# Attention keys, queries and weights turned by VectorE through DRAM instead of by TensorE

## The chip, the cores and the metric

The program runs on one core of a Trainium2 chip. The metric is the device time of one execution in microseconds, the median of three runs. One profiled execution of the kernel before gives the trace. The engines are TensorE (PE in the profile, with its weight loads as PEld), VectorE (DVE), ScalarE (ACT), GpSimd (POOL) and SyncE (SP). DMAs are issued from the queues of SP and ACT here.

## The reference

A context of 256 tokens and 256 latent tokens, width 2048, float32, two layers. What the change touches is the attention of the first layer, and the adaptive sums of both:

```python
def adaln(cond, w, b):
    m = jax.nn.silu(cond) @ w + b            # w is 2048 x 6144: one vector times a matrix
    return jnp.split(m, 3, axis=-1)
...
q = rms_norm(heads(cols(p, COL_Q, NA_WIDTH, 0), NA_HEADS, NA_HEAD_DIM), q_norm_g)   # 16 heads of 128
k = rms_norm(heads(cols(p, COL_K, NA_WIDTH, 0), NA_HEADS, NA_HEAD_DIM), k_norm_g)
...
s_lat = jnp.einsum('bqhd,bkhd->bhqk', qr, kb).astype(jnp.float32) * scale + bias.astype(jnp.float32)
s_ctx = jnp.einsum('bqhd,bkhd->bhqk', qr, k_ctx).astype(jnp.float32) * scale
pr = jax.nn.softmax(jnp.concatenate([s_lat, s_ctx], axis=-1), axis=-1).astype(v.dtype)
return (jnp.einsum('bhqk,bkhd->bqhd', pr[..., :kh * GRID_W], vb)
        + jnp.einsum('bhqk,bkhd->bqhd', pr[..., kh * GRID_W:], v_ctx))
...
ya = ya * jax.nn.silu(cols(p, COL_GATE_A, NA_WIDTH, 0))
```

Beside it the first layer has a state-space part (SSD) with a group norm; both go through one output projection, the second layer is a gated short convolution, and each layer ends with `x + gate * y`.

## The kernel before, in words

Nearly all of the work is projections. A float32 weight block of 128 x 1024 is loaded into one of five `raw` buffers by a DMA on the SP queue (`issue`), ScalarE casts it to a rounded high part `wH` (`split`, L423), VectorE subtracts to get the low part `wL` (`low_part`, L430), and TensorE multiplies high by high, high by low and low by high. There are three `wH`/`wL` pairs, so the split runs at most three blocks ahead of TensorE. `give_raw` hands a `raw` buffer back when its block is split, and the next load goes out.

The attention runs beside the projections in four groups `a` of four heads. `kq_gen` normalizes keys (4 tiles of 128 tokens x 4 heads of 128) and queries (2 tiles), and turns each 128 x 128 piece on TensorE (`turn`, L202: a matmul against the identity into a PSUM bank), from where ScalarE copies it to `KT` or VectorE, times `gqk`, to `QT`. `head_gen` makes scores with the splits `kH`, `kL`, `qH`, `qL`, adds the bias and takes the maximum in `top`, takes the exponential on ScalarE, scales by the sum in `scale_`, turns the weights of each 128 queries on TensorE in `trans` (4 pieces), splits them into `PH`, `PL`, and multiplies by the values. `put_mix` writes the head's output to DRAM (`mixd`), and `mix_gen` reads pairs of outputs back and splits them for the output projection.

`gemv_gen` forms the adaptive vectors: 16 blocks of 512 columns, each summed in `acc` by VectorE from 8 loads of `ada_w` (two operations of 128 x 512 each, L820), then summed over partitions by TensorE and written to `mrow`. These loads use the same SP queue and the same `raw` buffers as the weights. `res_gen` forms `x + gate * y` after the output projection, and `turn_gen` turns the result on TensorE.

The second layer already turns two tensors through DRAM: a tile is written with its 32 x 32 blocks reordered (`mixed`, `plain`), `fetch` reads it back in four DMAs on the ACT queue (L212) so that each block lands on its partitions, and `blocks` turns every 32 x 32 block on VectorE (L217). These are the tiles `Du` and `Dg` from the DRAM tensor `trd`.

The order of all instructions is fixed when the program is built. Tasks are generators in three lists (`urgent`, `side`, `back`); each yields a wait, `W_(engine, tiles, banks)`, and `pump` runs a task on when `may` says that by the planner's clock (`Plan`) its inputs are ready. `Plan.add` gives every instruction a start and an end by a table of costs; `when` waits for a condition, `("grow", t, h)` and `("cap", t, h)` take and return temporary buffers. "AQ" stands for a DMA on the ACT queue. The planner's clock only sets the order: on the chip each engine runs its own list in order and waits on semaphores. A DMA's issue waits too, in its queue.

Of the kernel before, what the change touches and what calls it, by code (L numbers as in the profile page):

```python
# [8 lines left out]
F32 = mybir.dt.float32  # L9
# [28 lines left out]
class Plan:  # L38
# [59 lines left out]
    def add(self, b):  # L98
# [8 lines left out]
        for k in ko:  # L107
            s = max(s, 0.0 if e == "PE" else self.w[k] + 60, self.r[k] + 60)
        if op == "DMACopy":
# [20 lines left out]
        for k in ko:  # L130
            self.w[k] = done
            self.last[k[0]] = max(self.last[k[0]], done)
# [9 lines left out]
def kernel(ctx: ExitStack, tc, x, cx, ada_w, ada_b, w_in, w_out, sc_in, sc_out, rpb, small, const,  # L142
# [120 lines left out]
    def may(task, hor, isurg):  # L263
# [48 lines left out]
    def force(ok, qs=(urgent, side)):  # L312

        pump()
        while not ok():
            best = None
            for q in qs:
                for task in list(q):
# [10 lines left out]
                    else:  # L329
                        if len(free_b) < nb:  # L330
                            continue
                        when_ = max(plan.t["ACT" if eng == "AQ" else eng], plan.ready(f))
# [472 lines left out]
    def gemv_gen():  # L805
        for n in range(16):
            lay = 0 if n < 4 else 1
            c0 = 4096 + n * 512 if n < 4 else (n - 4) * 512
            yield W_("DVE", nb=0)
            E(V.memset(acc, 0.0))  # L810
            E(DMA.dma_start(acc[:1, :], ada_b[lay:lay + 1, c0:c0 + 512]))
            for k in range(8):
                yield when(lambda: not (("gem", n, k) not in RAW))
                yield W_("DVE", RAW["gem", n, k][1], acc)
                raw, v = RAW.pop(("gem", n, k))
                ngem[0] -= 1
                for j in range(2):
                    if j:
                        yield W_("DVE", acc)
                    E(V.scalar_tensor_tensor(out=acc, in0=v[:, j], scalar=csil[:, 2 * k + j:2 * k + j + 1], in1=acc,  # L820
# [8 lines left out]
            E(V.tensor_copy(rowb, ps[:, :128]))  # L829
# [15 lines left out]
    rowb = mrb = st([128, 128], "rowb")  # L845

# [88 lines left out]

    def put_mix(i, o):
        yield W_("AQ", o)
# [7 lines left out]
    attn = [0]  # L945

    def kq_gen(key, a, ps, nt, stat, dst, banked):
# [10 lines left out]
        kns = {}  # L958

        def norm(t):  # L960
            kn = kns[t] = tmp()
            E(V.tensor_tensor(out=four(kn), in0=ps[t].rearrange("p (h d) -> p h d", h=4),
                              in1=stat[:, 4 * t:4 * t + 4].unsqueeze(2).to_broadcast([128, 4, 128]), op=ALU.mult))
            if banked:
                give(free_b, ps[t])

        for t in range(nt):
            yield W_("DVE", stat)
            norm(t)
        yield when(lambda: not (attn[0] < 8 * (a if key else 0)))  # L970
        for t in range(nt):
            yield W_("PE", kns[t], nb=1)
# [3 lines left out]
            give(free_t, kns[t])  # L976
            yield W_("ACT" if key == "K" else "DVE", pt)
            if key == "K":
                E(S.copy(dst[:, :, t * 128:(t + 1) * 128], four(pt)))
            else:  # L980
                E(V.tensor_scalar(out=dst[:, :, t * 128:(t + 1) * 128], in0=four(pt), scalar1=gqk, scalar2=None, op0=ALU.mult))
            give(free_b, pt)
# [24 lines left out]
    PH, PL = (st([128, 4, 256], f"PT{k}", F32R, name=f"P{'HL'[k]}") for k in range(2))  # L1007
# [4 lines left out]
    def head_gen(a, h):  # L1012
# [21 lines left out]
        def top(qt, ps):  # L1034
# [6 lines left out]
            E(S.activation(sp, sp, AF.Exp, bias=s4[:, 2 + qt:3 + qt], scale=1.0, accum_out=s4[:, 4 + qt:5 + qt]))  # L1041

        def scale_(qt):
            sp = sps[qt]
            E(V.reciprocal(s4[:, 6 + qt:7 + qt], s4[:, 4 + qt:5 + qt]))
            E(V.tensor_scalar(out=sp, in0=sp, scalar1=s4[:, 6 + qt:7 + qt], scalar2=0.5, op0=ALU.mult, op1=ALU.mult))

        def trans(qt):
            pt = bank()
            for kt in range(4):  # L1050
                turn(pt[:, kt * 128:(kt + 1) * 128], sps[qt][:, kt * 128:(kt + 1) * 128])
            give(free_t, sps[qt])
            return pt

        yield when(lambda: ("K", a) in got and ("Q", a) in got and (hd == 0 or ("qk", hd - 1) in got))
        yield ("grow", 2, 0)
        yield W_("ACT", KT[:, h, :], QT[:, h, :])
        E(S.copy(kH, KT[:, h, :]))
        E(S.copy(qH, QT[:, h, :]))
# [869 lines left out]
```

## Time and profile before

| what | value |
|---|---|
| median of three runs | 1801.51 us (1799.98 to 1804.06) |
| the profiled execution | 1802.22 us, its span 1800.3 us |
| busy, of the span | TensorE 98%, VectorE 71%, ScalarE 44%, GpSimd 2% |
| moved from and to HBM | 385.23 MB, mean 214 GB/s |
| granted TensorE clock | 0.998 |

A row of grouped instructions reads: line, engine, operation, output<-inputs, shapes, count | busy us, mean ns of one | idle us of the engine just before them, and what ended it. A row of a timeline reads: start, length, engine, line, operation, output<-input, shape, count, and in brackets the idle time before it with what ended it. A row of a table by stretch reads: stretch, length, then for each engine busy us and count, the granted TensorE clock, the share of time that the 16 DMA engines were busy, GB/s.

### The profile page before, as it was taken

The page shows a single profiled execution, that of the slowest core. Times are in us where ns is not written, and L with a number is a line of the kernel's source. Part 1 is how long each engine was busy: PE and PEld are TensorE (multiplying, and loading weights), DVE is VectorE, ACT ScalarE, POOL GpSimd, SP SyncE. Part 2 cuts the span into 40 slices and gives each one's busy share as a digit, 9 for nine tenths or more (in the row PEclk, how much of TensorE's full clock was granted, in tenths as well). Part 3 has the DMA queues.
Part 4 walks back from the last instruction along what each step waited for, and adds up shares of the span by engine and source line. Part 5 has one row for each costly group of instructions (what it writes and reads, how often), then busy time and mean ns, then how long its engine had stood idle before and what let it go on. Part 6 is the DMA issues. An engine that isn't in the chain of part 4 may idle for free.

```text
span 1800.3 us, 25545 instructions
## 1 busy us (share of the span) xinstructions
PE 1760.2 (98%) x9545; PEld 1469.2 (82%) x9545; DVE 1283.5 (71%) x2049; ACT 785.7 (44%) x1354; POOL 31.1 (2%) x28
## 2 busy tenths in 40 slices
PE   6999999999999999999999999999999999999998
PEld 4677888889888879888878898788877888878887
DVE  5566777878686867685875787787657777767555
ACT  5323544436252455242454343554445444434442
POOL 0000100001000000000001000000000000000000
PEclk9999999999999999999999999999999999999999
DMA  9987654576656556655574566768757888878774
GB/s 347 340 291 254 194 168 126 156 206 194 211 161 190 162 174 204 191 158 167 172 219 120 163 188 194 232 209 295 273 184 232 260 278 268 270 237 265 220 220 167
DMA packets 260220, 385.23 MB, mean 214 GB/s; under 512 B 33424, under 2 KB 113008, under 8 KB 260096
## 3 DMA queue, kind: packets, MB, share of 16 engines
q1 hardware_dynamic: 239792, 366.64, 64.8%
q10 hardware_dynamic: 20304, 16.96, 3.1%
q8 instruction: 75, 1.23, 0.3%
q14 instruction: 49, 0.40, 0.1%
HBM read 372.89 MB, written 11.96 MB: 214 GB/s over the span
## 4 chain that ended last, share of the span: by engine, by line
PE 89%; DMA 4%; DVE 4%; issue 1%; ACT 1%; SPq 0%; POOL 0%; ACTq 0%; POOLq 0%; DVEq 0%
PE bank L198 86%; PE bank L202 3%; DMA raw<-in_ada_w 2%; DVE wL L430 2%; DMA tmp<-dram_csr 1%; DVE acc L820 0%; DMA raw<-in_w_in 0%; DMA Dg<-dram_trd 0%; ACT wH L423 0%; DMA tmp<-in_x 0%; DMA xs<-in_x 0%; DVE hL L769 0%; DVE tmp L1398 0%; DVE tmp L1217 0%; DMA Du<-dram_trd 0%
## 5 line engine op out<-in xcount | busy, mean ns | idle before, releaser
L423 ACT CAST wH<-raw 128x1024 fp32r<-128x1024 f32 (+1 forms) x440 | 459.5, 1045 | 707.4 <-PE bank L198 606.5
L430 DVE TENSOR_TENSOR wL<-raw,wH 128x1024 fp32r<-128x1024 f32 (+1 forms) x440 | 530.5, 1212 | 225.9 <-ACT wH L423 224.1
L198 PE MATMUL bank<-hH,wH 128*128 128x256 f32 (+1 forms) x1040 | 342.7, 330 | 0.9 <-ACT wH L423 0.9
L198 PE MATMUL bank<-hL,wH 128*128 128x256 f32 (+1 forms) x1040 | 336.8, 324 | 0.0
L198 PE MATMUL bank<-hH,wL 128*128 128x256 f32 (+1 forms) x1024 | 331.3, 324 | 1.5 <-DVE wL L430 1.5
L198 PE MATMUL bank<-wH,h 128*128 128x512 f32 x1024 | 318.7, 392 | 2.1 <-DVE h L1662 1.7
L198 PE MATMUL bank<-wH,hH 128*128 128x512 f32 x640 | 257.2, 402 | 4.8 <-ACT hH L763 2.6
L820 DVE SCALAR_TENSOR_TENSOR acc<-raw,csil,acc 128x512 f32<-128x512 f32 x256 | 191.7, 749 | 91.0 <-DMA raw<-in_ada_w 74.0
L198 PE MATMUL bank<-wL,hH 128*128 128x512 f32 x640 | 249.8, 391 | 0.3 <-DVE wL L430 0.3
L198 PE MATMUL bank<-wH,hL 128*128 128x512 f32 x640 | 249.5, 390 | 0.1
L198 PEld LDWEIGHTS bank<-wH,h 128*128 128x128 f32 x1024 | 193.0, 189 | 44.3 <-DVE h L1662 3.0
L198 PEld LDWEIGHTS bank<-hH,wH 128*128 128x128 f32 x1040 | 197.6, 190 | 18.7 <-issue 2.0
L198 PEld LDWEIGHTS bank<-hL,wH 128*128 128x128 f32 x1040 | 197.7, 190 | 15.6
L198 PEld LDWEIGHTS bank<-hH,wL 128*128 128x128 f32 x1024 | 194.5, 190 | 17.8 <-DVE wL L430 2.5
L198 PE MATMUL bank<-wL,h 128*128 128x512 f32 x512 | 200.7, 392 | 5.4 <-DVE wL L430 5.4
L198 PE MATMUL bank<-wH,mix 128*128 128x512 f32 x512 | 162.7, 393 | 0.0
L198 PEld LDWEIGHTS bank<-wH,hH 128*128 128x128 f32 x640 | 120.2, 188 | 35.3 <-issue 6.5
L198 PEld LDWEIGHTS bank<-wH,hL 128*128 128x128 f32 x640 | 120.1, 188 | 25.6 <-DVE hL L769 0.6
L198 PEld LDWEIGHTS bank<-wL,hH 128*128 128x128 f32 x640 | 120.2, 188 | 24.8 <-DVE wL L430 1.1
L198 PEld LDWEIGHTS bank<-wL,h 128*128 128x128 f32 x512 | 96.6, 189 | 27.1 <-DVE wL L430 6.9
L198 PEld LDWEIGHTS bank<-wH,mix 128*128 128x128 f32 x512 | 96.1, 188 | 20.8 <-issue 0.9
L198 PE MATMUL bank<-wL,mix 128*128 128x512 f32 x256 | 99.8, 390 | 0.0
(257 smaller groups left out, 1754.4 us busy)
## 6 DMA issues: line engine op xcount, KB each, us to landing
raw<-in_w_in SPq DMA_DIRECT2D x209, 512.0 KB, 3.8
raw<-in_ada_w SPq DMA_DIRECT2D x163, 512.0 KB, 4.7
raw<-in_sc_in SPq DMA_DIRECT2D x128, 512.0 KB, 4.4
raw<-in_w_out SPq DMA_DIRECT2D x64, 512.0 KB, 4.8
raw<-in_sc_out SPq DMA_DIRECT2D x32, 512.0 KB, 4.6
tmp<-dram_csr SPq DMA_DIRECT2D x32, 256.0 KB, 6.2
PT<-in_ada_w SPq DMA_DIRECT2D x14, 512.0 KB, 8.0
yi<-in_ada_w SPq DMA_DIRECT2D x8, 512.0 KB, 7.4
```

The costliest lines, as they stand in the source:

```text
L198: E(T.matmul(o, l, r, start=start, stop=stop, skip_group_check=True))
L202: E(T.transpose(o, i, ident if k == 128 else ident[:k, :k]))
L423: E(S.copy(H, v))
L430: E(V.tensor_tensor(out=Lo, in0=v, in1=H.bitcast(F32), op=ALU.subtract))
L820: E(V.scalar_tensor_tensor(out=acc, in0=v[:, j], scalar=csil[:, 2 * k + j:2 * k + j + 1], in1=acc, op0=ALU.mult, op1=ALU.add))
```

## The change

Keys, queries and attention weights are no longer turned on TensorE. `kq_gen` writes each normalized tile, blocks reordered, to a new DRAM tensor `kqd`, fetches two tiles at a time into `PT0` and turns the blocks on VectorE straight into `KT` and `QT`. In `head_gen` the exponential is written with its blocks reordered, ScalarE does the scaling by the sum, both tiles go to `ptd` in DRAM and come back in one `fetch` into the same `PT0` (one user at a time, `dfree`), VectorE turns them in place, and `PH`, `PL` are made by one instruction each of 128 x 1024. `gqk` moves into the making of `qH`, `qL`, and the factor 0.5 into the product with the gate. In the group norm the matmul of ones against a scaled identity (`dg`) becomes a `turn` of a broadcast column. `put_mix` keeps an output in SBUF where its place is already free. The adaptive sums start by a product instead of a memset, and the bias `ada_b` is added at the end from `adab`. In the planner a DMA from or to DRAM tensors of the program is put down as 3 us longer, and a wait marked "+" (the adaptive sums, the turns, the splits of `mix_gen`) asks for 1 us more than the plan's ready time. `res_gen` starts only when all heads and groups are done.

```diff
@@ Plan.add
+            if any(a.tensor.name.startswith("dram") for a in ins + outs):
+                done = free = done + 3000
...
@@ may
+        late = eng[-1] == "+"
+        eng = eng.rstrip("+")
...
-        rdy = plan.ready(aps)
+        rdy = plan.ready(aps) + (1000 if late else 0)
...
@@ gemv_gen
-            yield W_("DVE", nb=0)
-            E(V.memset(acc, 0.0))
-            E(DMA.dma_start(acc[:1, :], ada_b[lay:lay + 1, c0:c0 + 512]))
+            yield W_("SP")
+            E(DMA.dma_start(adab[0:128:32, :], ada_b[lay, c0:c0 + 512].rearrange("(g c) -> g c", g=4)))
...
-                yield W_("DVE", RAW["gem", n, k][1], acc)
+                yield W_("DVE+", RAW["gem", n, k][1])
...
+                    if not k + j:
+                        E(V.tensor_scalar(out=acc, in0=v[:, j], scalar1=csil[:, 0:1], scalar2=None, op0=ALU.mult))
+                        continue
...
-            E(V.tensor_copy(rowb, ps[:, :128]))
+            E(V.tensor_tensor(out=rowb, in0=ps[:, :128], in1=adab, op=ALU.add))
...
@@ kq_gen
+            E(V.tensor_tensor(out=mixed(kn), in0=plain(ps[t]),
+                              in1=stat[:, 4 * t:4 * t + 4].unsqueeze(2).unsqueeze(3).to_broadcast([128, 4, 4, 32]), op=ALU.mult))
...
+            yield W_("AQ", kn)
+            E(DMA2.dma_start(src[t * 128:(t + 1) * 128], kn))
...
-            pt = bank()
-            for h in range(4):
-                turn(pt[:, h * 128:(h + 1) * 128], kns[t][:, h * 128:(h + 1) * 128])
...
-                E(S.copy(dst[:, :, t * 128:(t + 1) * 128], four(pt)))
...
-                E(V.tensor_scalar(out=dst[:, :, t * 128:(t + 1) * 128], in0=four(pt), scalar1=gqk, scalar2=None, op0=ALU.mult))
...
+        for t in range(0, nt, 2):
+            yield when(lambda: dfree[0])
+            Dk = d_take(f"kqD_{key}{a}{t}")
+            yield W_("AQ", src[t * 128:(t + 2) * 128])
+            fetch(Dk, src[t * 128:(t + 2) * 128])
+            for k in range(2):
+                yield W_("DVE+", Dk)
+                blocks(dst[:, :, (t + k) * 128:(t + k + 1) * 128], Dk[:, k])
+            dfree[0] = True
...
@@ head_gen
-            E(V.tensor_scalar(out=sp, in0=sp, scalar1=s4[:, 6 + qt:7 + qt], scalar2=0.5, op0=ALU.mult, op1=ALU.mult))
-
-        def trans(qt):
-            pt = bank()
-            for kt in range(4):
-                turn(pt[:, kt * 128:(kt + 1) * 128], sps[qt][:, kt * 128:(kt + 1) * 128])
...
+            E(S.mul(sps[qt], sps[qt], s4[:, 6 + qt:7 + qt]))
+            yield W_("AQ", sps[qt])
+            E(DMA2.dma_start(ptd[hd, qt * 128:(qt + 1) * 128], sps[qt]))
...
+        Dt = d_take(f"D{hd}")
...
+        fetch(Dt, ptd[hd])
+        for qt in range(2):
+            yield W_("DVE+", Dt)
+            turned = Dt[:, qt].rearrange("p (a k j) -> p a k j", a=4, k=4)
+            E(V.transpose(turned, turned))
...
-            mm(po[:, :256], vH[:, ks], PH[:, kt, :], kt == 0, False)
+            mm(po[:, :256], vH[:, ks], PH[:, :, kt, :], kt == 0, False)
...
@@ group_gen
-            mm(Rb[:, t * 128:(t + 1) * 128], ONES, dg[:, t * 128:(t + 1) * 128], t == 0, True)
+            turn(Rb[:, t * 128:(t + 1) * 128], r2[:, t:t + 1].to_broadcast([128, 128]))
```

How the rows move is shown at three places. A row names the line, the operation, output<-inputs with buffer numbers, the shape and how often it stands in succession.

First, TensorE while it projects the gate of head group 2 (`hH`, `hL` are the activations, `wH`, `wL` the weights, `tmp` the normalized keys). Before:

```order
L202 MATMUL bank4_127<-const_153,tmp0_104 128x128 x4
L198 MATMUL bank6_129<-hH10_1128,wH1_137 128x256
L198 MATMUL bank6_129<-hL10_1133,wH1_137 128x256
L198 MATMUL bank6_129<-hH10_1128,wL1_140 128x256
L198 MATMUL bank6_129<-hH10_1128,wH1_137 128x256
L198 MATMUL bank6_129<-hL10_1133,wH1_137 128x256
L198 MATMUL bank6_129<-hH10_1128,wL1_140 128x256
L202 MATMUL bank7_130<-const_153,tmp2_106 128x128 x4
L202 MATMUL bank3_126<-const_153,tmp7_111 128x128 x4
L198 MATMUL bank5_128<-hH11_1135,wH1_137 128x256
L198 MATMUL bank5_128<-hL11_1140,wH1_137 128x256
L198 MATMUL bank5_128<-hH11_1135,wL1_140 128x256
```

The same block of weights after the change:

```order
L200 MATMUL bank5_128<-hH10_1129,wH1_137 128x256
L200 MATMUL bank5_128<-hL10_1134,wH1_137 128x256
L200 MATMUL bank5_128<-hH10_1129,wL1_140 128x256
L200 MATMUL bank5_128<-hH10_1129,wH1_137 128x256
L200 MATMUL bank5_128<-hL10_1134,wH1_137 128x256
L200 MATMUL bank5_128<-hH10_1129,wL1_140 128x256
L200 MATMUL bank6_129<-hH11_1136,wH1_137 128x256
L200 MATMUL bank6_129<-hL11_1141,wH1_137 128x256
L200 MATMUL bank6_129<-hH11_1136,wL1_140 128x256
L200 MATMUL bank6_129<-hH11_1136,wH1_137 128x256
```

The turns are gone and nothing stands in their place; in the whole program TensorE's turns of `tmp` go from 324 to 100.

Second, ScalarE's list at the keys of group 2, where the copies from PSUM to `KT` stood before:

```order
L979 COPY KT_142<-bank3_126 128x4x128
L423 CAST wH0_136<-raw4_135 128x1024
L979 COPY KT_142<-bank4_127 128x4x128
L979 COPY KT_142<-bank7_130 128x4x128
L979 COPY KT_142<-bank3_126 128x4x128
L1058 CAST kH_1687<-KT_142 128x512
L1059 CAST qH_1691<-QT_143 128x256
```

After the change the queue holds four writes to `kqd` and two fetches of four DMAs between the casts of weights:

```order
L996 DMA dram_kqd_1683<-tmp3_107 128x512
L996 DMA dram_kqd_1683<-tmp2_106 128x512
L427 CAST wH1_137<-raw1_132 128x1024
L996 DMA dram_kqd_1683<-tmp6_110 128x512
L427 CAST wH2_138<-raw4_135 128x1024
L427 CAST wH0_136<-raw3_134 128x1024
L996 DMA dram_kqd_1683<-tmp4_108 128x512
L214 DMA kqD_K20_5892<-dram_kqd_1683 32x8x128 x4
L1024 ACTIVATE tmp7_111<-bank6_129 128x512
L1024 ACTIVATE tmp1_105<-bank5_128 128x512
L427 CAST wH1_137<-raw1_132 128x1024
L427 CAST wH2_138<-raw4_135 128x1024
```

VectorE's list for the same fetch after the change:

```order
L434 TENSOR_TENSOR wL0_139<-raw3_134,wH0_136 128x1024
L826 SCALAR_TENSOR_TENSOR acc_219<-raw0_131,csil_160,acc_219 128x512 x2
L1026 SCALAR_TENSOR_TENSOR gt_145<-tmp7_111,bank6_129 128x512
L1026 SCALAR_TENSOR_TENSOR gt_145<-tmp1_105,bank5_128 128x512
L434 TENSOR_TENSOR wL1_140<-raw1_132,wH1_137 128x1024
L835 TENSOR_TENSOR rowb_220<-bank0_123,adab_221 128x128
L219 STREAM_TRANSPOSE KT_142<-kqD_K20_5892 128x4x4x32 x2
L434 TENSOR_TENSOR wL2_141<-raw4_135,wH2_138 128x1024
```

The turn of the fetched tile stands one split behind the block (`wH0`) that ScalarE cast just ahead of the fetch and ahead of the split of `wL2`.

Third, VectorE in the second layer, where the third tile `Du` is turned (at 1595 us in the trace of before). Before:

```order
L810 MEMSET acc_219 128x512
L430 TENSOR_TENSOR wL1_140<-raw1_132,wH1_137 128x1024
L820 SCALAR_TENSOR_TENSOR acc_219<-raw3_134,csil_160,acc_219 128x512 x2
L430 TENSOR_TENSOR wL2_141<-raw2_133,wH2_138 128x1024
L820 SCALAR_TENSOR_TENSOR acc_219<-raw2_133,csil_160,acc_219 128x512 x2
L430 TENSOR_TENSOR wL0_139<-raw4_135,wH0_136 128x1024
L430 TENSOR_TENSOR wL1_140<-raw0_131,wH1_137 128x1024
L430 TENSOR_TENSOR wL2_141<-raw1_132,wH2_138 128x1024
L217 STREAM_TRANSPOSE u_10728<-Du2_12257 128x4x4x32 x2
```

After:

```order
L826 SCALAR_TENSOR_TENSOR acc_219<-raw3_134,csil_160,acc_219 128x512
L434 TENSOR_TENSOR wL2_141<-raw1_132,wH2_138 128x1024
L826 SCALAR_TENSOR_TENSOR acc_219<-raw3_134,csil_160,acc_219 128x512
L434 TENSOR_TENSOR wL0_139<-raw0_131,wH0_136 128x1024
L434 TENSOR_TENSOR wL1_140<-raw4_135,wH1_137 128x1024
L434 TENSOR_TENSOR wL2_141<-raw2_133,wH2_138 128x1024
L826 SCALAR_TENSOR_TENSOR acc_219<-raw3_134,csil_160,acc_219 128x512 x2
L434 TENSOR_TENSOR wL0_139<-raw1_132,wH0_136 128x1024
L434 TENSOR_TENSOR wL1_140<-raw0_131,wH1_137 128x1024
L219 STREAM_TRANSPOSE u_10688<-Du2_12207 128x4x4x32 x2
```

Before, `raw2` is freed by the split of `wL2` and its next load is used by the very next row, so that row has to wait for a whole load. After, three splits stand between the last use of `raw3` and the sum on its next load.

More of the change, by code (lines that the diff above doesn't have):

```diff
@@ L934, with place @@
     mixd = drt([32, 128, 256], "mixd")
-    def put_mix(i, o):
+    mH = [None] * 32
+    def place(i, o):
+        hl = st([128, 2, 256], f"hH{i}" if i < 16 else f"hL{i - 16}", F32R, name=f"mix{i}")
+        E(S.copy(hl[:, 0], o))
+        E(V.tensor_tensor(out=hl[:, 1], in0=o, in1=hl[:, 0].bitcast(F32), op=ALU.subtract))
+        mH[i] = hl
+    def put_mix(i, o):
+        if free_rows[0] > i % 16:
+            yield W_("ACT", o)
+            place(i, o)
+            give(free_h, o)
+            return
         yield W_("AQ", o)
@@ L1547 @@
     for k in range(3):
[L1548 removed]
+        spawn(urgent, mixes(k))
     do_gv(3, 4)
```

123 lines of the change are left out of this document (61 added, 62 removed).

## The prediction

> **What bounds the kernel now.** I read the page's busy times, then the chain of work that ended last, then TensorE's own waits, then the stretch in which the change lies.
>
> ```profile
> PE 1760.2 (98%) x9545; PEld 1469.2 (82%) x9545; DVE 1283.5 (71%) x2049; ACT 785.7 (44%) x1354; POOL 31.1 (2%) x28
> PE 89%; DMA 4%; DVE 4%; issue 1%; ACT 1%; SPq 0%; POOL 0%; ACTq 0%; POOLq 0%; DVEq 0%
> 215.00:1195.00 980.00, 974.78 (x5596) 838.88 (x5595) 740.42 (x1280) 435.82 (x847) 22.54 (x14) 1.00 0.60 178
> PE bank L198 <- DMA raw<-in_ada_w: 12.9, 2, 12.7
> PE bank L198 <- DVE wL L430: 7.2, 7, 4.4
> PE bank L198 <- ACT hH L763: 2.6, 2, 1.4
> ```
>
> TensorE is the bound: busy 98% of the span, 89% of the chain. The third row is the table by stretch for 215 to 1195 us, which holds every turn that the change removes: TensorE 974.8 of 980 us, VectorE 740, ScalarE 436, the DMA engines 0.60. So in this stretch a microsecond taken from TensorE's list is a microsecond off the time, as long as no other engine makes it wait; only 5.2 us of waiting are there now. The last three rows are TensorE's largest waits (total, times, longest): 12.9 us for the first loads, which the change doesn't touch, and 7.2 us for weight splits, of which one wait is 4.4.
>
> **The change: the turns.** A turn's price is not its duration. Group row and timeline of a set of four, then of a pair of the group norm's matmuls:
>
> ```profile
> L202 PE MATMUL bank<-const,tmp 128*128 128x128 f32 x324 | 45.9, 273 | 0.2 <-ACT KT L979 0.2
> 700.75 0.28 PE L198 MATMUL bank<-hL,wH 128*128 128x256 f32 x1
> 700.88 0.28 PE L198 MATMUL bank<-hH,wL 128*128 128x256 f32 x1
> 701.00 0.60 PE L202 MATMUL bank<-const,tmp 128*128 128x128 f32 x4
> 701.35 0.36 PE L198 MATMUL bank<-hH,wH 128*128 128x256 f32 x1
> 701.55 0.28 PE L198 MATMUL bank<-hL,wH 128*128 128x256 f32 x1
> 420.08 0.28 PE L198 MATMUL bank<-hH,wL 128*128 128x256 f32 x1
> 420.21 0.60 PE L198 MATMUL bank<-half,const 128*128 128x128 f32 x4
> 420.77 0.28 PE L198 MATMUL bank<-hL,wH 128*128 128x256 f32 x1
> ```
>
> Matmuls of 256 columns start 0.12 us apart (700.75, 700.88). From 700.88 to 701.55 are 0.67 us for two of them and four turns, so four turns cost 0.67 - 0.24 = 0.43 us. The change removes 24 tiles of keys and queries and 32 of attention weights, 56 sets of four (324 turns of `tmp` become 100): 56 x 0.43 = 24.1 us. The pair against `dg` is four records and costs 0.69 - 0.24 = 0.45; two turns instead are half a set, 0.22, so 8 groups save 8 x 0.23 = 1.8 us. No row shows a turn of a broadcast column; between nothing saved and 1.8 I take 1.8, since a turn loads a 128 x 128 operand either way. Together 25.9 us.
>
> The Trainium skill (TensorE: Matmul & The Clock Gate, Part 4: PE-mode transpose) puts a transpose in a kernel at about 275 ns; the row's mean of 273 agrees, but the starts 0.11 us apart say that they overlap. By the page's figure the 224 turns would be 61.6 us, an estimate, where starts give 24.1.
>
> The attention product now reads `PH` and `PL` in runs of 32 columns instead of 256 in a row: 3 x 4 x 16 = 192 matmuls of 256 columns at 0.12, 23 us in all. The nearest rows are matmuls of the time-step sums, which read two runs of 32 of a wider tile, beside such of 64 in a row:
>
> ```profile
> L198 PE MATMUL bank<-half,half 128*128 128x64 f32 x4 | 0.6, 260 | 0.0
> L198 PE MATMUL bank<-half,const 128*128 128x64 f32 x8 | 1.2, 268 | 0.0
> ```
>
> No penalty there (260 against 268 ns), so I take 0; the other end is twice the time, +23 us.
>
> **VectorE and ScalarE.** What comes and goes there, by like rows:
>
> ```profile
> L217 DVE STREAM_TRANSPOSE cg<-Dg 128x512 f32<-128x512 f32 x8 | 5.2, 688 | 1.5 <-DMA Dg<-dram_trd 1.5
> L217 DVE STREAM_TRANSPOSE u<-Du 128x512 f32<-128x512 f32 x8 | 5.2, 687 | 0.6 <-DMA Du<-dram_trd 0.6
> L1046 DVE TENSOR_SCALAR tmp<-tmp,s 128x512 f32<-128x512 f32 x32 | 15.6, 487 | 1.1
> L981 DVE TENSOR_SCALAR QT<-bank,gqk 128x512 f32<-128x512 f32 x8 | 5.8, 743 | 0.8 <-PE bank L202 0.8
> L820 DVE SCALAR_TENSOR_TENSOR acc<-raw,csil,acc 128x512 f32<-128x512 f32 x256 | 191.7, 749 | 91.0 <-DMA raw<-in_ada_w 74.0
> L810 DVE MEMSET acc<- 128x512 f32 x16 | 7.8, 485 | 0.9
> L1441 DVE TENSOR_SCALAR half<-const,r 128x128 f32<-128x128 f32 x16 | 3.9, 283 | 4.3 <-POOL r L1437 4.3
> L613 ACT ACTIVATE xs<-xs,rx 128x512 f32<-128x512 f32 x8 | 5.5, 717 | 4.6 <-POOL rx L572 4.6
> L979 ACT COPY KT<-bank 128x512 f32<-128x512 f32 x16 | 8.9, 589 | 8.7 <-PE bank L202 8.7
> ```
>
> VectorE gains 56 block turns: 56 x 0.688 = 38.5 us. It loses 15.6 (scaling) + 5.8 (`QT`) + 7.8 (memset) + 3.9 (`dg`) = 33.1, and 16 first sums become plain products, 16 x (749 - 487) ns = 4. Net +1 us of 1283: VectorE's load stays, only its order changes. The 16 splits `PL` of twice the size replace 32, no change. ScalarE gains 32 scalings, 32 x 0.717 = 22.9, and loses 16 copies, 9.4: +13.5 us, hidden in 544 idle us of the stretch. Writing the exponential with its blocks reordered has no row on ScalarE; at worst it doubles, another 23 us, hidden likewise.
>
> **The way through DRAM.** The same fetch stands in the second layer:
>
> ```profile
> q10 hardware_dynamic: 20304, 16.96, 3.1%
> dram_trd<-tmp ACTq DMA_DIRECT2D x16, 256.0 KB, 4.7
> Du<-dram_trd ACTq DMA_DIRECT2D x16, 128.0 KB, 8.1
> 1546.26 2.85 ACTq L212 DMA_DIRECT2D Dg<-dram_trd  x4
> 1403.97 1.84 ACTq L212 DMA_DIRECT2D Du<-dram_trd  x4
> ```
>
> 56 writes of 256 KB and 28 fetches of 512 KB are 29.4 MB; 8 writes and 4 reads of `mixd` less are -2.1. The ACT queue's 16.96 MB took 3.1% of 1800.3 = 55.8 us of all 16 engines, so 27.3 MB take 90 us, and the share in the stretch goes from 0.60 to about 0.69: no bound. On ScalarE's queue stand 156 DMAs more, at 1.84 to 2.85 us per four 72 to 111 us: 436 + 13 + 111 = 560 of 955, so a cast due in between is late by at most a fetch's 2.85 us, with three `wH` buffers of 12 or more matmuls each (2.7 us at 0.23 apart, as the rows of the stall below show) ahead. That cover gone, TensorE would wait for `wH`. Latency is what could show: a tile takes 4.7 us out and 8.1 back, and the splits of weights stand behind its turn on VectorE, with SP's next loads behind them. In the second layer 8 such fetches cost VectorE 1.5 + 0.6 = 2.1 us, with no 3 us in the plan; 28 would cost 7.4 by that row, all of it TensorE's if nothing covered it. The other end is that the 5.2 us of waits now in the stretch vanish. I take +1, nearest to the row, since most of a VectorE wait is covered by splits made ahead.
>
> The Trainium skill (VectorE: DVE Perf Modes, Rules for kernel authors) says to turn 128 x 128 on TensorE where PSUM will do, and so speaks against this change; by rows too the new way is dearer (0.688 us and a 13 us trip against 0.43), but on engines that idle.
>
> **The stall that goes.** At the third place shown of VectorE's list:
>
> ```profile
> 1584.44 1.22 DVE L430 TENSOR_TENSOR wL<-raw,wH 128x1024 fp32r<-128x1024 f32 x1
> 1590.66 1.54 DVE L820 SCALAR_TENSOR_TENSOR acc<-raw,csil,acc 128x512 f32<-128x512 f32 x2 [5.00 <-DMA raw<-in_ada_w]
> 1588.16 0.39 PE L198 MATMUL bank<-wL,h 128*128 128x512 f32 x1
> 1588.39 0.61 PE L198 MATMUL bank<-wH,h 128*128 128x512 f32 x2
> 1593.39 0.80 PE L198 MATMUL bank<-wL,h 128*128 128x512 f32 x1 [4.38 <-DVE wL L430]
> 1593.00:1597.00 4.00, 3.61 (x9) 2.84 (x10) 3.82 (x5) 0.00 (x0) 0.00 (x0) 0.50 0.91 300
> 1597.00:1601.00 4.00, 4.00 (x16) 3.23 (x15) 1.45 (x2) 2.53 (x5) 0.00 (x0) 0.84 0.59 224
> ```
>
> VectorE waits 5.0 us for a load whose buffer the row before freed; TensorE then idles 4.38 us, and its clock is 0.50 in the next 4 us: 9 matmuls where 3.61 us at 0.23 (1588.16 to 1588.39) hold 16, 7 x 0.23 = 1.6 lost, and some 2 (0.4 us) after that. 6.4 us. With three splits between, the load has its time; I take all 6.4, at the other end nothing.
>
> **The sum.** 1802.2 (profiled execution, 0.7 above the median) - 25.9 - 6.4 + 1.0 = 1770.9; against the median 1770.2, so 1770.
>
> **Rivals.**
> The cover is thin: VectorE stands at turned tiles for the full 7.4 us, TensorE with it, and a stall like that at 1590 comes back elsewhere. 1801.5 - 25.9 + 7.4 = 1783. For it: splits queue behind each turn; against: 2.1 us in 8.
> Slower than before: a tile is so late, held by ScalarE's queue, that TensorE idles over 4 us and its clock halves, 6.4 us each time. With the stall of 1590 mended, 32.3 / 6.4: from the sixth of 28 fetches on it is slower; with seven 1769.2 + 45 = 1814. Against it: the seven waits for `wL` now hold one such. The Trainium skill (TensorE: Matmul & The Clock Gate, Part 1) sets one idle window of about 3.4 us as what halves the clock; the row of 4.38 us agrees.
> Split reads of `PH` cost double: 1770 + 23 = 1793.
> Each turn frees its 273 ns: 224 x 0.273 = 61.2, so 1770.2 + 24.1 - 61.2 = 1733. Starts 0.11 apart speak against it.
> The turns are gone but the time isn't, since loads bound the stretch: within 0.2% of before. A DMA share of 0.60 speaks against it.
>
> **Chances.** Forecast 0.70, thin cover 0.15, split reads 0.05, 273 ns 0.02, nothing 0.03, slower 0.05. Best case: with the 5.2 us of waits gone too and no new one, 1769.2 - 5.2 = 1764, and 1 less for the spread of the runs; the range reaches to the thin cover and a little beyond: 1763 to 1786. Faster by over 0.2%, about what a measurement can tell: 0.92; same 0.03; slower 0.05.
>
> **What would show it.** Turns of `tmp` x100 in place of 324, TensorE's busy time near 1760.2 - 25.9 - 2 = 1732, VectorE's within 5 us of 1283; block turns of `KT`, `QT` and `D` with under 8 us of waiting for DMAs; the attention's matmuls still at 280 ns; no wait of TensorE over 3 us behind the first 25 us, and no slice of the clock below 9. It is wrong if TensorE's waits for `wL` or `wH` in 200 to 1200 us exceed 10 us, or if ScalarE's casts wait behind DMA issues.

## The result, and the profile after

The changed kernel takes 1792.8 us (median of 8 runs, 1786.7 to 1793.7) against 1803.9 us before (8 runs, 1800.0 to 1810.0): a ratio of 0.9927, 95% interval 0.9913 to 0.9942. It is faster, but by 11 us where the prediction had 32, and the time lies above its range. The profiled execution took 1792.6 us, its span 1790.8.

From the page of the changed kernel: busy time, the granted clock in 40 slices, the DMAs of ScalarE's queue, and the chain that ended last.

```profile
PE 1740.9 (97%) x9305; PEld 1450.0 (81%) x9305; DVE 1280.6 (72%) x2017; ACT 797.5 (45%) x1354; POOL 32.6 (2%) x29
PEclk9999999999999999999999999999999999999999
q10 hardware_dynamic: 56592, 44.24, 8.3%
PE 75%; DMA 10%; DVE 8%; issue 2%; ACT 2%; ACTq 1%; POOL 1%; SPq 0%; DVEq 0%; POOLq 0%
```

TensorE's share of the chain fell from 89% to 75%, and what took its place are DMAs (4% to 10%) and VectorE (4% to 8%). The page's clock line says nothing: every slice of 45 us shows 9. The table by stretch, with narrow stretches placed behind the waits, shows it (columns as before: TensorE, its loads, VectorE, ScalarE, GpSimd, clock, DMA share, GB/s):

```profile
215.00:1195.00 980.00, 959.99 (x5375) 822.16 (x5375) 753.61 (x1283) 448.88 (x854) 24.50 (x15) 0.99 0.71 210
200.00:1250.00 1050.00, 1029.13 (x5744) 880.90 (x5743) 798.72 (x1337) 483.34 (x932) 28.32 (x16) 0.99 0.72 215
237.40:240.70 3.30, 3.24 (x17) 2.95 (x16) 2.44 (x5) 0.00 (x0) 0.00 (x0) 0.50 0.91 282
316.00:322.60 6.60, 5.55 (x26) 5.55 (x27) 6.50 (x8) 0.66 (x1) 0.00 (x0) 0.50 0.66 218
459.00:465.00 6.00, 6.00 (x28) 4.96 (x27) 4.47 (x7) 1.05 (x1) 0.00 (x0) 1.00 0.82 245
947.40:950.70 3.30, 3.30 (x12) 2.65 (x9) 3.27 (x7) 1.38 (x5) 0.00 (x0) 0.50 0.39 134
```

In 200 to 1250 us TensorE idles 20.9 of 1050 us; the same stretch of before has 5.9:

```profile
200.00:1250.00 1050.00, 1044.08 (x5969) 897.82 (x5969) 787.69 (x1348) 471.92 (x931) 27.05 (x16) 1.00 0.62 186
```

The clock is halved four times, 17.1 us in all: at 237, 244, 316 (twice as long) and 947 us. TensorE's timeline, the six longest waits in this stretch:

```profile
236.34 0.39 PE L200 MATMUL bank<-hH,wL 128*128 128x256 f32 x1 [2.83 <-DVE wL L434]
243.31 0.66 PE L204 MATMUL bank<-const,tmp 128*128 128x128 f32 x4 [1.94 <-ACT tmp L1150]
317.05 0.58 PE L200 MATMUL bank<-hH,wL 128*128 128x256 f32 x1 [5.35 <-DVE wL L434]
458.20 0.43 PE L204 MATMUL bank<-const,r 128*128 128x128 f32 x2 [1.79 <-POOL r L1467]
943.77 0.43 PE L200 MATMUL bank<-tmp,xtm 128*64 128x128 f32 x2 [1.25 <-DVE tmp L1431]
946.42 0.65 PE L200 MATMUL bank<-tmp,xtm 128*64 128x128 f32 x6 [2.21 <-DVE tmp L1431]
```

Take TensorE's busy time and subtract half of what lies in stretches at half clock; the rest is its work at full clock:

| us | before | after | change |
|---|---|---|---|
| TensorE's work at full clock | 1757.7 | 1733.0 | -24.8 |
| lost to the halved clock | 2.4 | 7.9 | +5.5 |
| TensorE idle | 40.1 | 49.9 | +9.8 |
| span | 1800.3 | 1790.8 | -9.5 |

So the work went as forecast, and waits took most of it back. The chain behind the wait at 236 us, in the timelines of ScalarE, VectorE and SP:

```profile
223.68 3.58 ACTq L214 DMA_DIRECT2D kqD_K<-dram_kqd  x4
230.85 0.34 ACTq L996 DMA_DIRECT2D dram_kqd<-tmp  x1
231.24 0.78 ACT L1241 ACTIVATE tmp<-bank,cbh,cwh 128x512 f32<-128x512 f32 x1 [7.00 <-DMA kqD_K<-dram_kqd]
231.92 1.98 ACT L427 CAST wH<-raw 128x1024 fp32r<-128x1024 f32 x2
...
225.83 0.75 DVE L826 SCALAR_TENSOR_TENSOR acc<-raw,csil,acc 128x512 f32<-128x512 f32 x1
232.05 3.10 DVE L1247 SCALAR_TENSOR_TENSOR tmp<-bank,cwh,tmp 128x508 f32<-128x508 f32 x4 [5.48 <-ACT tmp L1241]
235.07 2.35 DVE L434 TENSOR_TENSOR wL<-raw,wH 128x1024 fp32r<-128x1024 f32 x2
...
222.09 3.79 SPq L397 DMA_DIRECT2D raw<-in_w_in  x3
225.94 10.14 SPq L1045 DMA_DIRECT2D bias<-dram_rpbs  x8
```

ScalarE issues a fetch of keys, and then a write, which can't be issued before 230.85. The activation behind it starts 7.0 us late, VectorE stands 5.5 us for that activation, the split `wL` stands behind VectorE's convolution, and TensorE waits for the split. At the same time SP needs 10 us to issue eight small loads of biases.

The row at 231.24 puts the 7.0 us down to the fetch. The semaphores (counters that a DMA raises as it lands) say more, with their times in the trace: the write waits for semaphore 109, which a load of weights had taken (the second of SP's three in the row at 222.09, issued at 224.13), and which that load counted up for the last time at 230.77. So ScalarE stood there for a weight load of SP's queue, and not for its own fetch. What holds the queues is in the built program: the DMAs of SP and ScalarE take eight semaphores (`DMAHW0` to `DMAHW7`) in turn, and an issue waits for the DMA that had its semaphore before. In the trace, too, the DMAs of both queues use the same eight semaphores. ScalarE's list from the built program, with the waits of the same fetch:

```
L214 DMA kqD_K00_1860<-dram_kqd_1683 32x8x128 [waits DMAHW6_49,DMAHW3_49]
L214 DMA kqD_K00_1860<-dram_kqd_1683 32x8x128
L214 DMA kqD_K00_1860<-dram_kqd_1683 32x8x128 [waits DMAHW2_49]
L214 DMA kqD_K00_1860<-dram_kqd_1683 32x8x128 [waits DMAHW4_49]
```

Eight DMAs can be under way, of both queues together; a fetch takes four of the places, and the plan doesn't know of them. By the semaphores' times, ScalarE's issues stood 31 us for another DMA in 200 to 1250 us, 25 of these for loads that SP had issued; before the change, not at all.

All five of TensorE's waits over 1.7 us lead back to such a place: those at 236 and 243 us to the write at 230.85; that at 317 to a fetch of attention weights that stood until 308.41 for a load of `ada_w`; that at 458 to a write that stood until 452.90 for a load of biases; that at 946 to a fetch of queries that stood until 939.52 for a load of `ada_w` issued at 929.22.

The profile's own table counts more, since ScalarE's time for issuing is idle time in it: waits of ScalarE that a DMA ended sum to 94.0 us in the same stretch (44.2 before), and it puts 40.8 of them down to DMAs of `kqd` and `ptd`. The three largest of these (total, times, longest):

```profile
ACT half L1447 <- DMA kqD_Q<-dram_kqd: 14.2, 2, 8.7
ACT wH L427 <- DMA kqD_K<-dram_kqd: 11.3, 2, 6.5
ACT tmp L1241 <- DMA kqD_K<-dram_kqd: 7.0, 1, 7.0
```

The Trainium skill (DMA: Bandwidth & Descriptors, Anatomy of one DMA) says that DMA engines don't wait on semaphores; the issuing sequencer waits before dispatch. The 7.00 us at 231.24 agree: the wait of a DMA is a wait of ScalarE.

### The profile page after: what moved, and what is told of

Same layout as the page of the kernel before. It is cut to its first block, busy times and chain, and to the rows that moved or that the text cites. A ratio compares the mean times of both kernels' runs of the same rounds, so it can differ in the third digit from the quotient of the medians.

```text
span 1790.8 us, 25262 instructions
## 1 busy us (share of the span) xinstructions
PE 1740.9 (97%) x9305; PEld 1450.0 (81%) x9305; DVE 1280.6 (72%) x2017; ACT 797.5 (45%) x1354; POOL 32.6 (2%) x29
## 4 chain that ended last, share of the span: by engine, by line
PE 75%; DMA 10%; DVE 8%; issue 2%; ACT 2%; ACTq 1%; POOL 1%; SPq 0%; DVEq 0%; POOLq 0%
PE bank L200 74%; DMA raw<-in_ada_w 4%; DVE wL L434 3%; PE bank L204 1%; DVE acc L826 1%; ACT wH L427 1%; DMA raw<-in_w_in 1%; DMA tmp<-dram_mixd 1%; DMA Du<-dram_trd 1%; DMA kqD_K<-dram_kqd 1%; ACTq L214 1%; DMA dram_ptd<-tmp 1%; DMA bias<-dram_rpbs 1%; DVE tmp L1247 1%; POOL statk L576 0%
## 5 line engine op out<-in xcount | busy, mean ns | idle before, releaser
L200 PEld LDWEIGHTS bank<-hH,wL 128*128 128x128 f32 x1024 | 197.1, 192 | 25.7 <-DVE wL L434 10.2
L826 DVE SCALAR_TENSOR_TENSOR acc<-raw,csil,acc 128x512 f32<-128x512 f32 x240 | 179.5, 748 | 39.4 <-DMA raw<-in_ada_w 35.5
L200 PEld LDWEIGHTS bank<-wH,mix 128*128 128x128 f32 x512 | 96.1, 188 | 20.9 <-ACT Vt L1015 0.6
```

The source lines that it names most:

```text
L200: E(T.matmul(o, l, r, start=start, stop=stop, skip_group_check=True))
```

## The experiments

Theory A: DMA issues that wait hold ScalarE's queue, and casts and activations behind them come late. Rival B: the waits come from the new rules of the plan and the adaptive sums. Rival C: turned tiles simply land later than planned. Later came rivals D (the plan's new rule helps any version), E (GpSimd issues too slowly) and F (the chance of the order). The margin is what the plan adds for a transfer through DRAM; "rule" is the plan of e4, "GpSimd" the fetches of e6. The ratio is to the kernel before on the same chip; as that took 1802.4 to 1806.5 us on the chips used here, small differences between runs are to be read from the ratios. The last columns are from the profiled execution: TensorE's idle time in 200 to 1250 us, and the time at half clock there.

| run | turns through DRAM | margin ns | also | us | ratio | 95% interval | idle | half clock |
|---|---|---|---|---|---|---|---|---|
| before | none | | | | 1 | | 5.9 | 0 |
| after | all | 3000 | | 1792.8 | 0.9927 | 0.9913 to 0.9942 | 20.9 | 17.1 |
| e1 | weights | 3000 | | 1785.0 | 0.9883 | 0.9862 to 0.9904 | 9.0 | 3.4 |
| e2 | keys, queries | 3000 | | 1794.6 | 0.9934 | 0.9916 to 0.9952 | 11.5 | 3.4 |
| e3 | none | 3000 | | 1795.9 | 0.9939 | 0.9922 to 0.9957 | 6.4 | 0 |
| e4 | all | 3000 | rule | 1776.5 | 0.9832 | 0.9813 to 0.9852 | 10.4 | 13.7 |
| e5 | none | 3000 | rule | 1795.8 | 0.9947 | 0.9932 to 0.9962 | 8.2 | 0 |
| e6 | all | 3000 | GpSimd | 1783.4 | 0.9883 | 0.9866 to 0.9899 | 14.9 | 13.7 |
| e7 | weights | 3000 | rule | 1776.2 | 0.9838 | 0.9823 to 0.9853 | 1.9 | 0 |
| e8 | all | 6000 | | 1784.8 | 0.9891 | 0.9874 to 0.9908 | 14.2 | 6.8 |
| e9 | all | 2800 | | 1803.8 | 0.9990 | 0.9974 to 1.0006 | 25.4 | 30.7 |
| e10 | all | 3200 | | 1782.0 | 0.9864 | 0.9850 to 0.9878 | 12.5 | 6.8 |
| e11 | all | 3000 | rule, SP too | 1776.5 | 0.9831 | 0.9815 to 0.9848 | 11.7 | 6.8 |
| e12 | all but first keys, queries | 3000 | rule | 1777.8 | 0.9844 | 0.9830 to 0.9857 | 10.4 | 6.8 |
| e13 | all | 2800 | rule | 1785.0 | 0.9898 | 0.9884 to 0.9911 | 15.0 | 10.2 |
| e14 | all | 3200 | rule | 1784.6 | 0.9895 | 0.9881 to 0.9908 | 15.0 | 13.7 |
| e15 | all | 6000 | rule | 1847.2 | 1.0243 | 1.0229 to 1.0257 | 35.6 | 31.4 |
| e16 | none | 2800 | | 1793.7 | 0.9948 | 0.9935 to 0.9960 | 2.9 | 0 |
| e17 | all | 2800 | GpSimd | 1787.4 | 0.9904 | 0.9889 to 0.9919 | 14.6 | 13.7 |
| e18 | weights | 2800 | rule | 1786.4 | 0.9894 | 0.9878 to 0.9910 | 8.4 | 3.4 |

**e1 to e3: one part back, or both.**

```diff
@@ kq_gen (e1, e3)
-            E(DMA2.dma_start(src[t * 128:(t + 1) * 128], kn))
...
-                blocks(dst[:, :, (t + k) * 128:(t + k + 1) * 128], Dk[:, k])
+                turn(pt[:, h * 128:(h + 1) * 128], kns[t][:, h * 128:(h + 1) * 128])
@@ head_gen (e2, e3)
-        fetch(Dt, ptd[hd])
...
-            E(V.transpose(turned, turned))
+            pt = trans(qt)
```

> The changed kernel, with keys and queries turned by TensorE again (24 sets of four turns back); attention weights still go through DRAM, all else as changed. 24 x 0.43 = 10.3 us come back to TensorE. Theory A (a fetch holds ScalarE's queue: its DMA issues wait for DMAs issued before them, the casts and activations behind it come late, VectorE and then TensorE stand): of the waits of the changed kernel, those at 233 to 243 us (5.0 idle and 3.4 of clock), 458 us (1.8) and 944 to 946 us (3.5 and 1.7) follow fetches of keys or queries, 15 us in all; they go, so 1792.8 + 10.3 - 15 = 1788, range 1783 to 1796, and TensorE's idle time falls from 49.9 to about 40. Rival B (the waits come from the new rules of the plan and the adaptive sums, not from the fetches): the waits stay, 1803. Rival C (only the turned tiles' own lateness counts, VectorE standing at its block turns): VectorE's wait for key and query tiles is 7.6 us in the changed kernel, so at most 7.6 go, 1795.5 or more.

> The changed kernel, with the attention weights turned by TensorE again (32 sets of four back, scaling by VectorE, PH and PL in rows of 256); keys and queries still go through DRAM. 32 x 0.43 = 13.8 us come back. Theory A: of the long waits only that at 317 us (5.35 idle, 2.8 of clock) follows a fetch of attention weights, so 1792.8 + 13.8 - 8.2 = 1798, range 1793 to 1805; the waits near 235 and 945 us stay in some form. Rival B: 1806.6, all waits stay. Rival C: VectorE waits 2.0 us for turned weights, 1804.6.

> The changed kernel with both kinds of turns on TensorE again; what stays are the adaptive sums with their margin, the plan's rules, the group norm's turn of a broadcast column, the mix placed without DRAM. TensorE gets 24.1 us back. Theory A: no stall that halves the clock in 200 to 1200 us, TensorE idles about 6 us there as in the kernel before, and the stall at 1590 us stays mended: 1803.9 - 7.8 (stall and clock) - 1.8 (group norm) = 1794, range 1790 to 1800. Rival B: the stalls of 200 to 1000 us are there without the turns too, 1792.8 + 24.1 = 1817.

All three came within 4 us of theory A's values (within 6 by the ratios), against B's 1803, 1807 and 1817. TensorE's waits of e3 in 200 to 1240 us, in full:

```profile
PE bank L200 <- DVE wL L434: 4.5, 4, 1.7
PE bank L204 <- DVE tmp L1371: 1.0, 1, 1.0
PE bank L200 <- DVE tmp L1430: 0.5, 2, 0.3
PE bank L204 <- ACT KT L1007: 0.2, 1, 0.2
```

Without the turns through DRAM nothing over 1.7 us is left and the clock is never halved, with the same rules of the plan and the same adaptive sums; e5 and e16 below, two more orders without these turns, have no wait over 1.7 us there either. B falls. e1 and e2 prove less: each is a single order, and putting either part back took TensorE's idle time from 20.9 to 9.0 or 11.5 us, so the two parts don't add up. And e3 alone is 10 us faster than before: most of the gain that was measured is not that of the turns. Its TensorE time of 1757.2 us, none of it at half clock, against 1733.0 of work with the turns moved, gives 24.2 us for the turns.

**e4, e5 and e7: the plan counts DMAs.**

```diff
@@ Plan
+        self.ring = deque([0.0] * 8, 8)
...
         if op == "DMACopy":
+            s = max(s, self.ring[0])
...
+            self.ring.append(done)
@@ may, eng "AQ"; nd is 4 ahead of a fetch, else 1
-            return t <= now + hor and rdy <= t
+            return t <= now + hor and max(rdy, max(list(plan.ring)[:nd])) <= t
```

> The changed kernel with one more rule in its plan: a DMA issue of SP or ScalarE waits for the end of the DMA eight issues before it (of both queues together), and a write or a fetch through DRAM is put into the order only when that wait is over by the plan; a fetch needs four such places. Same instructions, other order. Theory A: the time that ScalarE stands at DMA issues (14.2 + 11.3 + 7.0 us at fetches of keys and queries alone) falls by half or more and TensorE's waits in 200 to 1240 us from 20.8 to under 10 us, with no or one halving of the clock: 1792.8 - 10 - 5 = 1778, range 1770 to 1787. Rivals B and C: no change beyond 3 us, 1790 to 1796.

> The third experiment's kernel (no turn through DRAM) with the fourth's rule in the plan (a DMA issue of SP or ScalarE waits for the DMA eight issues before). Control: is the fourth's gain one of the turns, or would the rule help any version? Theory A: without fetches there is little to mend, TensorE waits 6.4 us in 200 to 1240 us of the third: 1795.9 - 3 = 1793, range 1789 to 1798; then the turns through DRAM are worth 1793 - 1776.5 = 16.5 us once the plan counts DMAs. Rival D: the rule gives its 16 us without the turns as well, 1780, and the turns are worth 3 us at most.

> The fourth experiment's plan rule on the first's kernel: only the attention weights go through DRAM. 10.3 us of TensorE come back against the fourth; its waits at 233 to 236, 308 and 929 to 933 us (1.23 + 2.05 + 0.8 + 0.3 + 3.4 = 7.8 idle, and 5 us of halved clock, 2.6 lost... of 10.2 us at half) go if they are those of keys and queries: 1776.5 + 10.3 - 7.8 - 5.1 = 1774, range 1768 to 1783. If those waits come from elsewhere: 1787.

With the turns the rule brought 16 us (1776.5 for the 1778 expected), without them nothing (1795.8 and 1795.9): rival D falls. Keys and queries back on TensorE cost nothing (e7, 1776.2 for 1774), though TensorE does 10.3 us more. TensorE's waits of e7 in 200 to 1240 us are three rows:

```profile
PE bank L205 <- DVE tmp L1403: 0.7, 1, 0.7
PE bank L205 <- DVE half L1143: 0.6, 1, 0.6
PE bank L209 <- ACT KT L1014: 0.2, 1, 0.2
```

So in e7 all 32 sets of four are gained: its TensorE is busy 1741.5 us, that of e5 1756.0, 14.5 for the 13.8 by the prediction's price.

**e6: fetches issued by GpSimd. e8: a larger margin.**

```diff
@@ fetch (e6, e17), for kqd and ptd
-            E(DMA2.dma_start(dst[32 * b:32 * b + 32]...
+            E(G.dma_start(dst[32 * b:32 * b + 32]...
@@ Plan.add (e8; 2800 in e9, 3200 in e10)
-                done = free = done + 3000
+                done = free = done + 6000
```

> The changed kernel, with the fetches of turned keys, queries and weights (112 DMAs) issued by GpSimd instead of ScalarE; the writes stay on ScalarE, the plan has no new rule. Theory A: ScalarE is no longer held by a fetch; its waits at DMA issues of fetches (32.5 us for those of keys and queries) go, and so do the stalls of TensorE behind them: 1792.8 - 10 to 18, so 1779, range 1772 to 1788. Rival B (the order by the plan's new rules makes the stalls): 1790 to 1796. Rival E: GpSimd takes so long to issue a fetch that turned tiles come late, VectorE stands at them, and the time is over 1796.

> The changed kernel with 6000 ns instead of 3000 ns added to transfers through DRAM in the plan. Theory C (turned tiles come later than the plan thinks, and VectorE stands at them): VectorE's 7.6 and 2.0 us of waiting for them go, with the stalls behind, 1783 or less. Theory A: the plan still doesn't know what holds ScalarE; the order changes, the stalls move but don't go: 1787 to 1798.

e6 gained 9 us, the weak end of theory A. ScalarE's waits at DMAs of `kqd` and `ptd` went from 40.8 us to none, yet TensorE still idles 14.9 us. The longest, in its timeline and in VectorE's:

```profile
248.10 0.58 PE L200 MATMUL bank<-hH,wL 128*128 128x256 f32 x1 [4.62 <-DVE wL L434]
...
246.48 0.43 DVE L1167 TENSOR_TENSOR half<-half,half 128x256 f32<-128x256 f32 x1 [7.59 <-DMA half<-in_rows]
246.83 1.22 DVE L434 TENSOR_TENSOR wL<-raw,wH 128x1024 fp32r<-128x1024 f32 x1
```

Here it is a small load from SP's queue that comes late: the queue of ScalarE is one way for the lateness, not the only one. e6 also does two things at once: in its trace GpSimd's DMAs count on eight semaphores of their own, so the fetches leave the shared places as well as ScalarE's queue. e8 gained 8 us too, 1784.8: below A's 1787 to 1798, and just above C's 1783. Before reading anything into 8 us, two runs asked what a meaningless change does.

**e9 and e10: 200 ns less, 200 ns more.**

> The changed kernel with 2800 ns in place of 3000 in the plan for transfers through DRAM: a change too small to mean anything by itself, which gives another order. It measures how far the time moves by the order's chance alone. Theory A with chance: the waits of TensorE in 200 to 1240 us fall elsewhere and differ in number; 1792.8 give or take 5, and the 8 us of the margin of 6000 are then within that scatter. Theory C (lateness of turned tiles, so that a larger margin gains steadily): 2800 is no faster than 3000, 1792 to 1795.

> As the one before, with 3200 ns. Theory A with chance: 1792.8 give or take 5, not in order with the margin. Theory C: between 3000's 1792.8 and 6000's 1784.8, nearest the first: 1792.

1803.8 and 1782.0 us, beside 1792.8: twice the scatter expected. The three times fall as the margin grows, as C would have it, but by 11 us for 200 ns, and 6000 ns lies between them. VectorE's waits at fetched tiles aren't in that order either: 5.7 us in e9, 12.1 in the changed kernel, 4.6 in e10. So C doesn't set the time. But the total of A's waits doesn't rank the three any better: ScalarE's issues stood for another DMA for 19 us in e9, 31 in the changed kernel, 23 in e10. Why one order fares worse than another is not shown.

In e9 (six halvings; the seventh that an expectation counts begins 1.3 us before the end of the span) TensorE waits at 315 and 459 us as after, and at new places:

```profile
314.85 0.58 PE L200 MATMUL bank<-hH,wL 128*128 128x256 f32 x1 [5.12 <-DVE wL L434]
459.03 1.01 PE L200 MATMUL bank<-const,half 128*128 128x1 f32 x4 [3.15 <-DVE half L1454]
1127.93 1.12 PE L200 MATMUL bank<-tmp,xtm 128*64 128x128 f32 x6 [3.60 <-DVE tmp L1431]
```

Followed back like those of the changed kernel, its waits at 235, 315 and 459 us lead to an issue of ScalarE that stood for a load of SP. That at 1128 leads to a load of `ada_w` that was under way for 10.9 us and that VectorE's sums stood for, and that at 710 (1.8 us) to no DMA.

**e11 and e12: two tries to go on from e4.**

```diff
@@ may, eng "SP"; nd is 4 ahead of a head's bias loads (e11)
-            return rdy <= max(t, now) + 200
+            return max(rdy, max(list(plan.ring)[:nd])) <= max(t, now) + 200
@@ kq_gen (e12)
+        if a == 0:  # turns by TensorE, as in e1
```

> The fourth experiment's kernel, and now SP's tasks in the plan (four bias loads of a head, the adaptive bias, rows) also wait for a free place among the last eight DMAs. In the fourth SP took 11.2 us (224 to 235) to issue the first two heads' eight bias loads, ScalarE stood 8 us behind a fetch beside it, and TensorE's waits at 233 to 236 us follow. Theory A: these go (3.3 idle and 1.7 of clock): 1776.5 - 5 = 1771.5, range 1766 to 1779. If the place of the bias loads doesn't matter: 1776.

> The fourth experiment's kernel with the first group of four heads' keys and queries turned by TensorE, the other three groups' through DRAM: 6 sets of four, 2.6 us, come back. Every kernel so far with all keys through DRAM has TensorE waiting 2 to 5 us near 235 to 250 us, with the clock halved behind it. Theory A: that wait goes, the later ones stay: 1776.5 + 2.6 - 3.3 - 1.7 = 1774, range 1769 to 1780.

Neither moved the time: 1776.5 and 1777.8. The waits near 235 us went (to 1.6 us in e11, none in e12), and others of 2.4 and 2.7 us came at 424 us.

**e13 to e18: is it the rule, or luck?**

> The fourth experiment's rule with the margin of 2800 ns that gave 1803.8 us without it. Theory A (the stalls come from DMA issues that the plan doesn't foresee, and the rule foresees them): close to the fourth's 1776.5, range 1770 to 1784. Rival F (the order's chance alone: the fourth was a lucky order): anywhere from 1782 to 1804.

> The rule with 3200 ns (1782.0 without it). Theory A: 1776.5, range 1770 to 1784. Rival F: 1782 to 1804.

> The rule with 6000 ns (1784.8 without it). Theory A: 1776.5, range 1768 to 1784; if lateness of turned tiles is a cause beside the rule's, 1770. Rival F: 1782 to 1804.

> The third experiment's kernel (all turns by TensorE) with 2800 ns in place of 3000, no rule. Theory A: without fetches on ScalarE's queue the order's chance is small: 1795.9 give or take 3. Rival F: it scatters as the changed kernel does, 1795.9 give or take 11.

> The sixth experiment (fetches issued by GpSimd, no rule) with the margin of 2800 ns, which with fetches on ScalarE gave 1803.8 us and seven halvings of the clock. Theory A (ScalarE held by the fetches passes their lateness on to the casts): 1783 again, range 1776 to 1790, and no wait of ScalarE at a fetch. Rival F (order's chance, whatever queue): as likely 1782 as 1804.

> The seventh experiment (only the attention weights through DRAM, with the rule that counts DMAs; 1776.2 us and 1.5 us of TensorE waits in 200 to 1240 us) with 2800 ns. If the keys and queries carry the stalls: 1776 again, 1773 to 1781. If the seventh was a lucky order: 1782 to 1792.

Three things follow. First, the scatter comes with the turns: without them 1795.9 and 1793.7 us at two margins, with them 1803.8 to 1782.0 (though without them the margin touches only 184 DMAs between 200 and 1250 us, for 352). Second, by the ratios the rule took 17 us off at 2800 and at 3000 ns, and cost 6 at 3200 and some 63 at 6000. So it is no cure: e13 and e14, 1785.0 and 1784.6, lie just outside the 1770 to 1784 that A allowed and inside F's 1782 to 1804, and e15 is slower than either allowed. e4's 1776 was in part a lucky order. In e13 late tiles show as well, the way that C had in mind: VectorE stands 2.1 us for fetched queries before each of TensorE's two longest waits, 3.58 and 3.03 us at 666 and 935. The table by stretch of e15, and a wait in it:

```profile
1238.00:1300.00 62.00, 32.02 (x106) 24.60 (x106) 32.86 (x59) 20.77 (x33) 0.00 (x0) 0.64 0.48 139
1281.22 0.58 PE L205 MATMUL bank<-PH,vH 128*128 128x256 f32 x1 [12.94 <-ACT vH L1128]
```

With 6 us more for every trip, and every place in the ring held so long in the plan, the heads fall behind: the last four are turned at 1241 to 1287 us, where the last two of the changed kernel were at 1206 and 1221. By then little of the projections is left to run beside them, it seems, and TensorE works 32 of 62 us, at a clock of 0.64. Third, fetches by GpSimd gain at both margins (9.4 and 16.4 us), which fits that ScalarE's queue passes lateness on; but these are two orders beside a scatter of 22 us, and 14.9 and 14.6 us of idle time stay. Weights alone with the rule scatter too (1776.2, 1786.4: e7 was a lucky order as well), and at both margins keys and queries add nothing (1776.5 against 1776.2, 1785.0 against 1786.4).

The best kernels, e4, e7 and e11, take 1776 us, 0.983 to 0.984 of before and 0.99 of the changed kernel; their neighbours at 2800 and 3200 ns take 1785. Which share of the remaining waits comes from ScalarE's queue, from SP's, and from late tiles was not told apart; nor whether a plan could be had whose time doesn't hang on 200 ns.

## Why the prediction was wrong, step by step

- **Turns.** 24.1 us for 56 sets of four at 0.43: right, 24.2 by e3. Starts, not durations, priced these matmuls; the rival of 61 us was out. The pairs of the group norm: 1.8 was too much; TensorE's work in e3 (1757.2) is only 0.5 below before (1757.7).
- **Split reads of `PH`.** No price, as taken; the other end of 23 us was out. The first row is the kernel before, the others are groups of the changed kernel:

```profile
L198 PE MATMUL bank<-PH,vL 128*128 128x256 f32 x64 | 17.9, 279 | 0.0
L200 PE MATMUL bank<-PH,vL 128*128 128x256 f32 x64 | 18.4, 288 | 1.3 <-DVE vL L1123 1.3
L204 PE MATMUL bank<-const,tmp 128*128 128x128 f32 x100 | 15.6, 279 | 2.0 <-ACT tmp L1150 1.9
L219 DVE STREAM_TRANSPOSE KT<-kqD_K 128x512 f32<-128x512 f32 x16 | 10.5, 690 | 7.6 <-DMA kqD_K<-dram_kqd 7.6
L1109 DVE STREAM_TRANSPOSE D<-D 128x512 f32<-128x512 f32 x32 | 22.3, 702 | 4.5 <-DMA D<-dram_ptd 4.5
```

- **Work of the other engines.** VectorE -2.9 us for +1, ScalarE +11.8 for +13.5, a DMA share of 0.71 for 0.69, 8.3% on ScalarE's queue (149 us of all 16 DMA engines) for 146: right.
- **The stall at 1588 us.** Mended as said: 230 us from 1370 on hold 229.5 of work, and e3 keeps this without the turns. In idle time and clock it is 7.2 us for 6.4.
- **New waits, +1.0 between -5.2 and +7.4.** This step failed. They are 22.4 us: 15.0 more idle in 200 to 1250 us and 7.9 of clock, less 0.5 elsewhere. It was sized by VectorE standing at turned tiles, and that came out near the bound (7.6 + 4.5 = 12.1 us), but it is not what TensorE waited for.
- **The sentence that let it through** is that "a cast due in between is late by at most a fetch's 2.85 us". The issue time was read from fetches in the second layer, where an issue hardly waited. In the first layer an issue waits for earlier DMAs of both queues, and such a fetch holds ScalarE for up to 8.7 us (930 to 940 us, `kqD_Q`); 5.2 of these its last DMA stood for a load of `ada_w` that SP had issued. The built program listed those waits. The trace of before showed none: its largest wait of ScalarE that a DMA ended, 18.9 us in 14 pieces, was for `tmp<-dram_csr`, an input of the very activations that waited.
- **The price of a stall** was put at over 4 us of idle time. Of the six waits shown above, 1.94 us already had half clock behind it. With four halvings the rival that ended slower was the nearest in kind, and e9 is that rival but for its size: 25.4 us idle, 30.7 at half clock, and no gain at all. e9 differs from the changed kernel in the order alone, and the prediction gave the chance of the order no term.

Of the prediction's signs against it, ScalarE's casts behind DMA issues came, and so did a wait over 3 us and 12.1 us of VectorE at fetched tiles, where none and under 8 were to be. TensorE's waits for `wL` in 200 to 1250 us, 9.1 us in all, stayed just under the 10 that were to count against it. That no slice of the clock falls below 9 was no sign at all, since a slice is 13 times as long as a halving.

## What to carry to other kernels

Before moving work to a DMA, list what stands behind that DMA on its issuing engine and how many DMAs may be under way at once; with eight places for two queues, an issue costs what the oldest of eight has left, not what a quiet stretch shows. Where an order is laid down when the program is built, time two or three neighbours of a constant before believing a gain of under 1%: here 400 ns in a table moved the kernel by 22 us, and the parts that stayed the same in every neighbour (10 us without the turns) were the ones to trust. A gain on the bound engine is worth its waits: with the rule, keys and queries took 10.3 us off TensorE's work and nothing off the kernel's time, at two margins.

## What the runs showed of the chip

- The clock was halved in steps of 3.4 us (3.4, 6.8 or more), each 1.7 us of work lost. Which waits had one behind them, over all these traces from 200 us on and the clock full before the wait: of those that stood alone (no other wait over 0.4 us within 6.8 us), none of 36 between 1.3 and 1.7 us; one of six up to 1.8 (1.72 us in e17); six of the seven between 1.81 and 1.96; five of eight from 2.0 to 2.4; all 18 over 2.4 us. The rows above show both sides: 1.79 us at 458 with a clock of 1.00 behind it, 2.83 at 236 with 0.50. The Trainium skill (TensorE: Matmul & The Clock Gate, Part 1) gives an idle window of about 3.4 us; the step agrees, but here waits of about half of it were often enough, from 1.72 us on.
- The 112 DMAs of the fetches, issued by GpSimd, made it busy 99.8 us instead of 32.6 in e6, 0.6 us each, with VectorE's busy time the same (1279.8 against 1280.6).

```profile
PE 1738.4 (98%) x9305; PEld 1448.5 (81%) x9305; DVE 1279.8 (72%) x2017; ACT 799.3 (45%) x1354; POOL 99.8 (6%) x141
```
